# Identity matrix by a running sum, a matmul and a comparison, and reciprocal roots of two or three token tiles at once, in a one-core hybrid decoder step

## Chip, cores and metric

The kernel runs on one core of one Trainium2 chip. The metric is the device time of one execution in microseconds (us): 1366.59 us before, the median of 3 runs (1365.39 to 1371.83). One further execution was recorded by the hardware profiler; its trace is the source of all durations below. Engines: PE is TensorE (matmuls; PEld its weight loads), DVE is VectorE, ACT is ScalarE, POOL is GpSimd, SP is the queue that issues most DMAs.

## The reference, cut to what matters

One decoder layer over 1024 prompt tokens and 8 sample tokens of width 1024: an RMS norm, a wide input product, an S5 state-space branch and a convolution branch that are gated and merged, a SwiGLU feed-forward layer, and a last RMS norm.

```python
def rmsnorm(x, g):
    xf = x.astype(jnp.float32)
    y = xf * lax.rsqrt(jnp.mean(xf * xf, axis=-1, keepdims=True) + EPS)
    return (y * g.astype(jnp.float32)).astype(x.dtype)
...
    xn = rmsnorm(x, g_mix)
    z = xn @ w_in
    u = z[..., :D_SSM]
    ...
    y, hr, hi = s5_layer(u, h_re, h_im, a_re, a_im, log_dt, b_re, b_im, c_re, c_im, d)
    yg = jax.nn.gelu(y) @ w_glu
    ...
    x = x + merged @ w_out
    hn = rmsnorm(x, g_ffn) @ w_ff_in
    x = x + (jax.nn.silu(hn[..., :D_FF]) * hn[..., D_FF:]) @ w_ff_out
...
    return rmsnorm(x, g_final), ...
```

## The kernel before

**Tiles and stages.** The tokens stand in nine tiles `xt[0]` to `xt[8]`: eight of 128 tokens, and `xt[8]` with the 8 sample tokens. Products are made in float16 with a high and a low part of both sides (`wh`/`wl`, `xn` high and low), three matmuls for each. The stages by the profile: up to 84 us the first norm, the transposes of x and the product `u` (line 734, tile `pu`); then the rest of the input product together with S5 and the convolution branch; then the output product (line 1177), feed-forward (1291 and 1370), and from about 1331 us the last product (1391), a transposition of each token tile (1400) and the last norm.

**The order of work.** The program is recorded through a scheduler that simulates the engines and places each engine's instructions by readiness and priority (`hp()` raises it). The engines then run in that fixed order, each waiting for its own next instruction: a row of an engine that waits holds all rows behind it. Moving one dependency can so reorder rows of other parts.

**The identity.** `ident` is the first 128 columns of the tile `zi` (line 632 clears the rest). All transposes on TensorE multiply by it, and so wait for it. It was made by a library helper on GpSimd: a memset (masks.py:197) and an affine select (masks.py:199). `ones` (634) is a tile of ones, used by small matmuls that sum over partitions.

**The first norm.** `norm(ks)` squares each tile of a group on ScalarE with a running sum in a column of `ss` (705), makes a reciprocal root with `rsqrt` on VectorE (three scaled copies `rv` of the sum, a first guess `ry` by integer arithmetic, three rounds of Newton's method through `rt`: lines 615 to 626), and scales the tile (710 on VectorE for x0 and x1, 712 on ScalarE for the others). It is called for (0), (1), (2, 3), (4, 5) and (6, 7, 8). `xpose` transposes a group (724, tile `ptr`) and splits it into high and low halves of `xn` (608 on ScalarE, 609 on VectorE).

**The first weights.** `wscale_pe` takes the sums of squares of two weight tiles (516), adds them up on TensorE (546, `pws`) and makes a power of two `usc` (501) of it, with which `wsplit16` splits the weights (561 on ScalarE, 565 on VectorE). `raw` has two tiles at its first call. Later weights get their scale by an all-reduce over partitions on GpSimd (521, result `sv` read at 526 on VectorE).

**S5's loads.** `load_a` loads `ldt`, the step sizes, and `an`; `load_b` loads `cn`, `B`, `dn`, `h0n`; all are issued by GpSimd. `B` holds the same data in partitions 0 to 63 and 64 to 127: the upper half was copied from the lower. `prep(0)` makes an exponential of `ldt` on VectorE (lines 53 to 66, tiles `ex_x`, `ex_m`, `ex_p`).

**The last norm.** In three groups of token tiles (5 to 8, 0 to 2, 3 and 4), each tile in turn is transposed into `tr` (a PSUM pool with three buffers), squared with its sum (1403), given a reciprocal root of its own, and multiplied by that and the gain into `yo` (1410), which is stored.

Of the kernel before, what the change touches and what calls it, by code (L numbers as in the profile page):

```python
# [8 lines left out]

F32 = mybir.dt.float32  # L10
# [4 lines left out]
AF = mybir.ActivationFunctionType  # L15
ALU = mybir.AluOpType
MUL, ADD, SUB, MAXI, MINI = ALU.mult, ALU.add, ALU.subtract, ALU.max, ALU.min

P = 128
D = 1024  # L20
# [16 lines left out]
class S5:  # L37
# [54 lines left out]
    def load_b(self, dma):  # L92
        self.cn = []
        for i, c in enumerate((self.c_re, self.c_im)):
            t = self.t([P, 4, 2, NS], "^cn", tag="W", bufs=2)
            src = c[0].rearrange("(q g) c p -> (g c) q p", q=4)
            for r in range(2):
                dma.dma_start(t[:, :, r], src)
            self.cn.append(t)
        self.B = []  # L100
        for i, b in enumerate((self.b_re, self.b_im)):
            t = self.t([P, G, 16], f"B{i}")
            dma.dma_start(t[0:64], b[0].rearrange("g p c -> p g c"))
            dma.dma_start(t[64:128], t[0:64])
            self.B.append(t)
        self.dn = self.t([16, 512], "dn")
        dma.dma_start(self.dn, self.d[0:1, :].to_broadcast([16, 512]))
        self.h0n = self.t([P, 2, 3, NS], "^h0n", tag="E", bufs=2)
        for i, h in enumerate((self.sre, self.sim, self.sre)):
            dma.dma_start(self.h0n[:, :, i], h[0].rearrange("(q s) g p -> (s g) q p", q=2))  # L110
# [330 lines left out]
def hybrid_step(ctx: ExitStack, tc: tile.TileContext, x_prompt, x_sample, state_ssm_re, state_ssm_im,  # L441
# [4 lines left out]
    nc = tc.nc  # L446
    V, A, T, GP, SY = nc.vector, nc.scalar, nc.tensor, nc.gpsimd, nc.sync
# [3 lines left out]
    yk = y_p[0].rearrange("(j k) d -> k j d", k=8)  # L451
    xsm, ysm = x_sample[:, 0, :], y_s[:, 0, :]

    cp = ctx.enter_context(tc.tile_pool(name="cp", bufs=1))
    wp = ctx.enter_context(tc.tile_pool(name="wp", bufs=3))
    pa = ctx.enter_context(tc.tile_pool(name="pa", bufs=NA))
    ms = ctx.enter_context(tc.tile_pool(name="ms", bufs=2, space=bass.MemoryType.PSUM))
# [8 lines left out]
    def nm(s):  # L466
        uid[0] += 1
        return f"{s}_{uid[0]}"

    def sa(name, shape=(P, TOK), dt=F32):  # L470
        return pa.tile(list(shape), dt, name=nm(name), tag="a")

    def sb(name, shape=(P, TOK), dt=F32, tag="b"):
        return (pm if tag == "mg" else pb).tile(list(shape), dt, name=nm(name), tag=tag, bufs=NBT[tag])

    def hp():
        return tc.high_priority(offset=HPO)
# [36 lines left out]
    def sumsq(src, junk, o):  # L514
        with nc.allow_low_precision(reason="bound of a scale"):
            A.activation(junk, src, AF.Square, accum_out=o)  # L516
# [23 lines left out]
    def wscale_pe(raws, his):  # L540
        with tc.high_priority(offset=HPS):
            ss = cp.tile([P, 2], F32, name=nm("uss"), tag="uss", bufs=2)
            pt = pst.tile([P, 512], F32, name=nm("pws"), tag="pu")
            for i, raw in enumerate(raws):
                sumsq(raw, his[i].bitcast(BF16), ss[:, i:i + 1])
                T.matmul(pt[:, 0:1], ones, ss[:, i:i + 1], start=(i == 0), stop=(i == len(raws) - 1))
            v = cp.tile([P, 1], F32, name=nm("uv"), tag="uv", bufs=2)
            V.tensor_scalar(v, pt[:, 0:1], 1e-28, None, MAXI)
            o = cp.tile([P, 1], F32, name=nm("usc"), tag="usc", bufs=2)
            pow2(v, o, "pyw")  # L550
        return o
# [52 lines left out]
    def pair(t):  # L604
        return t[:, 0], t[:, 1]
# [5 lines left out]
    def rsqrt(ss, n, scale, r=P):  # L611
        v = cp.tile([P, 3, 9], F32, name=nm("rv"), tag="rv", bufs=2)[:r, :, :n]
        y = cp.tile([P, 9], I32, name=nm("ry"), tag="ry", bufs=3)[:r, :n]
        t = cp.tile([P, 9], F32, name=nm("rt"), tag="rt", bufs=2)[:r, :n]
        V.tensor_scalar(v[:, 0], ss, 64 * scale, 64 * EPS, MUL, ADD)
        V.tensor_scalar(y, v[:, 0].bitcast(I32), -0.5, -550020641.0, MUL, ADD)
        V.tensor_scalar(v[:, 1], ss, 16 * scale, 16 * EPS, MUL, ADD)
        V.tensor_scalar(v[:, 2], ss, 4 * scale, 4 * EPS, MUL, ADD)
        f = y.bitcast(F32)
        for i in range(3):  # L620
            if n == 1:
                V.scalar_tensor_tensor(t, f, f, v[:, i], MUL, MUL)
            else:
                V.tensor_tensor(t, f, f, MUL)
                V.tensor_tensor(t, t, v[:, i], MUL)
            V.scalar_tensor_tensor(f, t, -3.0, f, ADD, MUL)
        return f

    zi = cp.tile([P, 240], F32, name="zi")
    ident = zi[:, :P]  # L630
    make_identity(nc, ident)
    GP.memset(zi[:, P:], 0.0)
    ones = cp.tile([P, P], F32, name="ones")
    GP.memset(ones, 1.0)

    e5, e5c, e5t, est = ExitStack(), ExitStack(), ExitStack(), ExitStack()
    sp = e5.enter_context(tc.tile_pool(name="s5p", bufs=1, side="right"))
# [5 lines left out]
    xt = [None] * 9  # L643

    xn = []
    for _ in range(8):
        t = sa("xn", (P, 2, TOK), F16)
# [21 lines left out]
    raw = [wdma(w_in, 0, 8, P * m) for m in range(2)]  # L669
# [7 lines left out]
    pt = ms.tile([P, 512], F32, name="pgv", tag="ms")  # L677
# [10 lines left out]
    pt = ms.tile([P, 512], F32, name="pgm", tag="ms")  # L688
# [7 lines left out]
    def norm(ks):  # L696
        n = len(ks)
        with hp():
            ss = cp.tile([P, 3], F32, name=nm("ss"), tag="ss", bufs=2)
            if 8 in ks:  # L700
                GP.memset(ss, 1.0)
            junk = px.tile([P, D], BF16, name=nm("junk"), tag="junk", bufs=1)
            for i, k in enumerate(ks):
                r = P if k < 8 else 8
                A.activation(junk[:r], xt[k][:r], AF.Square, accum_out=ss[:r, i:i + 1])
            for i, k in enumerate(ks):
                r = P if k < 8 else 8
                f = rsqrt(ss[:, i:i + 1], 1, 1.0 / D)
                if k < 2:
                    V.tensor_scalar(xt[k], xt[k], f, None, MUL)  # L710
                else:
                    A.mul(xt[k][:r], xt[k][:r], f[:r])

    def cols(gr):
        return gr[0] * P, sum(P if k < 8 else 8 for k in gr)
# [42 lines left out]

    norm((0,))
    norm((1,))  # L760
    pairs = [wpair(), wpair()]
    wus = [wscale_pe(raw, [p[0] for p in pairs])]
    wui = [invs(wus[0], gxc[:, 1:2], "uinv", 2)]
    wu = [wsplit16(raw[0], *pairs[0], wus[0], parts=4)]
    xpose(groups[0])
# [6 lines left out]
    pairs = [[kt_(t, bufs=2) for _ in range(2)] for t in ("cosi", "M")]  # L772
# [163 lines left out]
    for m in range(4):  # L936
        t = sb("gyt")
# [100 lines left out]
    for c in range(3):  # L1038
        pt = ms.tile([P, 512], F32, name=nm("pmu"), tag="ms")
# [14 lines left out]
    for m in range(4):  # L1054
        a = acc[m]
# [19 lines left out]
    x1 = [None] * 8  # L1075
# [43 lines left out]
    for m in range(4):  # L1119
        h, l = pair(sb("chp", (P, 2, TOK), F16, tag="gy"))  # L1120
# [231 lines left out]
    for b in range(len(blocks) - 1):  # L1352
# [6 lines left out]
        for m in range(8):  # L1359
# [4 lines left out]
            for h in range(2):  # L1364
                pt = qpsum()
                for k in range(blocks[b]):
                    for q, (u, v) in enumerate(((0, 0), (0, 1), (1, 0))):
                        for z in range(2):
                            c0 = 516 * h + 258 * z
                            T.matmul(pt[:, z, :258], w[u][:, k], hid[k][v][:, c0:c0 + 258],  # L1370
                                     start=(k == 0 and q == 0), stop=(k == blocks[b] - 1 and q == 2))
# [9 lines left out]
    gf = sb("gf", (P, D), tag="gy")  # L1381
    SY.dma_start(gf, g_final[None, :].to_broadcast([P, D]))
    emq.close()
    tr = ctx.enter_context(tc.tile_pool(name="tr", bufs=3, space=bass.MemoryType.PSUM))
    for gr in ((5, 6, 7, 8), (0, 1, 2), (3, 4)):
        c0, w = cols(gr)
        for m in range(8):
            pt = ms.tile([P, 512], F32, name=nm("pfo"), tag="ms")
            for k in range(nb):
                for i, (a, b) in enumerate(((0, 0), (0, 1), (1, 0))):  # L1390
                    T.matmul(pt[:, :w], wl[m][a][:, k], hid[k][b][:, c0:c0 + w],
                             start=(k == 0 and i == 0), stop=(k == nb - 1 and i == 2))
            with hp():
                V.scalar_tensor_tensor(x1[m][:, c0:c0 + w], pt[:, :w], iwl[:, m // 2:m // 2 + 1], x1[m][:, c0:c0 + w],
                                       MUL, ADD)
        for k in gr:
            r = P if k < 8 else 8
            pt = tr.tile([P, 2, 512], F32, name=nm("tr"), tag="tr")
            for m in range(8):
                T.transpose(pt[:r, m // 4, (m % 4) * P:(m % 4 + 1) * P], x1[m][:, k * P:k * P + r], ident)  # L1400
            yo = sb("yo", (P, D))
            ss = cp.tile([P, 1], F32, name=nm("ss"), tag="ss", bufs=2)
            A.activation(yo[:r].rearrange("p (a b) -> p a b", a=2), pt[:r, 0:2], AF.Square,
                         accum_out=ss[:r, 0:1])
            f = rsqrt(ss[:r, 0:1], 1, 1.0 / D, r)
            dst = yk[k] if k < 8 else ysm
            step = 1 if k in (3, 4) else 2
            for h in range(0, 2, step):
                c = slice(512 * h, 512 * (h + step))
                V.scalar_tensor_tensor(yo[:r, c].rearrange("p (a b) -> p a b", a=step), pt[:r, h:h + step], f[:r, 0:1],  # L1410
                                       gf[:r, c].rearrange("p (a b) -> p a b", a=step), MUL, MUL)
                SY.dma_start(dst[:, c], yo[:r, c])


NA = 21
# [33 lines left out]
```

## Time and profile before

| | |
|---|---|
| median of 3 runs | 1366.59 us |
| the profiled execution | 1366.18 us |
| its span in the trace | 1364.1 us |
| granted TensorE clock, mean | 0.975 |
| instructions of the profile's VectorE | 2402 |
| loaded and stored by DMA | 96.66 MB |

The span runs from the first to the last recorded instruction; the execution's own time is 2.1 us longer. In the rows below a line number is that of the kernel before. `<-` between tiles reads "made from"; at the end of a row in brackets stands the idle time before it and what ended it. "issue" is time in which an engine waited for nothing that the profile shows. In the row of a DMA issue the last number is the time from issue to landing.

### The profile page before, as it was taken

The numbers are of one execution on the slowest core, as the hardware profiler recorded it, in microseconds if no ns is written. First come the engines' busy times: TensorE is split into PE (matmuls) and PEld (weight loads), VectorE is DVE, ScalarE is ACT, GpSimd is POOL, SyncE is SP. The second block draws the span as 40 slices with busy tenths as digits, with TensorE's granted clock in tenths as the row PEclk, the third lists the DMA queues.
The fourth block names the chain that finished last, engine by engine and source line by source line (L and its number), as shares of the span: only waits on it lengthen the run. The fifth ranks groups of instructions, "written<-read, shape, count | busy, mean of one in ns | idle before, by whom it ended". The sixth has DMA issues, their size and how long they took to land.

```text
span 1364.1 us, 25399 instructions
## 1 busy us (share of the span) xinstructions
PE 1263.1 (93%) x10083; PEld 1001.7 (73%) x10083; DVE 1036.5 (76%) x2402; ACT 621.6 (46%) x1118; POOL 102.8 (8%) x198
## 2 busy tenths in 40 slices
PE   3898797999998999799979999999999999999996
PEld 2776565666666666578658888888888888888884
DVE  5976788989997744768897857776785777678758
ACT  5843433453333545744354534444453544445522
POOL 5000012001110100000000000000000000000100
PEclk9899898999999999999979999999999999999998
DMA  6445665341122123410011121112112111221203
GB/s 190 130 97 120 135 113 119 81 127 50 48 62 63 30 82 98 135 32 1 17 41 46 40 78 48 40 55 68 50 39 78 48 39 55 68 58 32 77 18 125
DMA packets 169632, 96.66 MB, mean 71 GB/s; under 512 B 12927, under 2 KB 165643, under 8 KB 169513
## 3 DMA queue, kind: packets, MB, share of 16 engines
q1 hardware_dynamic: 168109, 92.44, 24.8%
q0 software_dynamic: 896, 1.63, 0.6%
q8 instruction: 79, 1.29, 0.4%
q10 hardware_dynamic: 507, 0.97, 0.3%
q14 instruction: 41, 0.33, 0.1%
HBM read 76.72 MB, written 9.65 MB: 63 GB/s over the span
## 4 chain that ended last, share of the span: by engine, by line
PE 51%; DVE 26%; issue 9%; DMA 8%; ACT 4%; POOL 1%; SPq 1%; DVEq 0%; ACTq 0%; POOLq 0%
PE q L1291 18%; PE q L1370 12%; PE mm L594 10%; PE q L1177 5%; DMA wr<-in_w_ff_in_dram 5%; DVE acc L898 4%; PE pu L734 2%; DVE ws L1249 2%; DVE wl L565 2%; DVE tb L898 1%; DMA Y<-X 1%; POOL sv L521 1%; ACT ws L1248 1%; DVE g L1270 1%; DVE mh L609 1%
## 5 line engine op out<-in xcount | busy, mean ns | idle before, releaser
L1291 PE MATMUL q<-xs,ws 128*128 128x258 f16 (+2 forms) x3696 | 422.6, 275 | 18.7 <-DVE xs L1225 6.7
L1291 PEld LDWEIGHTS <-ws 128*128 128x128 f16 x3696 | 358.4, 98 | 81.7 <-issue 24.6
L594 PEld LDWEIGHTS <-wh 128*128 128x128 f16 x1728 | 169.5, 98 | 86.2 <-issue 5.1
L594 PE MATMUL mm<-xn,wh 128*128 128x344 f16 (+2 forms) x1152 | 203.8, 311 | 1.9 <-ACT ut L746 1.1
L1370 PE MATMUL q<-hp,wh 128*128 128x258 f16 x1280 | 193.5, 272 | 0.0
L521 POOL PARTITION_ALL_REDUCE sv<-wss x110 | 71.0, 646 | 936.0 <-ACT wh L516 510.7
L1370 PEld LDWEIGHTS <-wh 128*128 128x128 f16 x1280 | 124.0, 97 | 18.1
L561 ACT ACTIVATE wh<-wr,wsc 128x512 f16<-128x512 f32 (+1 forms) x76 | 70.0, 922 | 126.9 <-DVE wsc L501 122.6
L1370 PE MATMUL q<-hp,wl 128*128 128x258 f16 x640 | 122.5, 273 | 0.0
L594 PE MATMUL mm<-xn,wl 128*128 128x344 f16 (+2 forms) x576 | 118.0, 312 | 0.0
L594 PEld LDWEIGHTS <-wl 128*128 128x128 f16 x864 | 85.2, 99 | 41.3 <-issue 0.3
L516 ACT ACTIVATE wh<-wr 128x512 bf16<-128x512 f32 (+1 forms) x78 | 65.0, 833 | 107.6 <-PE q L1370 44.6
L516 ACT ACTIVATE junkw<-wr 128x1024 bf16<-128x1024 f32 x52 | 54.8, 1054 | 109.2 <-DMA wr<-in_w_ff_in_dram 101.6
L565 DVE SCALAR_TENSOR_TENSOR wl<-wr,wsc,wh 128x512 f16<-128x512 f32 (+1 forms) x76 | 75.9, 999 | 22.6 <-ACT wh L561 22.4
L1374 DVE SCALAR_TENSOR_TENSOR x<-q,inv,x 128x516 f32<-128x516 f32 x80 | 59.9, 750 | 35.8 <-PE q L1370 35.6
L1177 PE MATMUL q<-mh,wo 128*128 128x258 f16 x672 | 80.0, 275 | 7.5 <-ACT mh L608 4.2
L1249 DVE SCALAR_TENSOR_TENSOR ws<-sw,wsc,ws 128x512 f16<-128x512 f32 x88 | 64.7, 744 | 19.4 <-ACT ws L1248 18.4
L1177 PEld LDWEIGHTS <-wo 128*128 128x128 f16 x672 | 64.3, 96 | 19.9 <-issue 7.6
L1248 ACT ACTIVATE ws<-sw,wsc 128x512 f16<-128x512 f32 x88 | 62.3, 715 | 28.9 <-PE q L1291 28.8
L1370 PEld LDWEIGHTS <-wl 128*128 128x128 f16 x640 | 61.9, 97 | 9.0
L594 PE MATMUL mm<-gyp,wh 128*128 128x344 f16 x384 | 66.6, 309 | 1.4 <-DVE mg L971 0.8
L1249 DVE SCALAR_TENSOR_TENSOR ws<-wr,wsc,ws 128x512 f16<-128x512 f32 x66 | 48.7, 744 | 17.9 <-ACT ws L1248 17.6
(404 smaller groups left out, 1852.8 us busy)
## 6 DMA issues: line engine op xcount, KB each, us to landing
wr<-in_w_ff_in_dram SPq DMA_DIRECT2D x44, 512.0 KB
wr<-in_w_in_dram SPq DMA_DIRECT2D x28, 512.0 KB
wr<-in_w_ff_out_dram SPq DMA_DIRECT2D x44, 256.0 KB
xt<-in_x_prompt_dram SPq DMA_DIRECT2D x8, 512.0 KB
cosi<-pc SPq DMA_DIRECT2D x32, 128.0 KB
wr<-in_w_glu_dram SPq DMA_DIRECT2D x16, 256.0 KB
wr<-in_w_out_dram SPq DMA_DIRECT2D x8, 512.0 KB
xc<-in_x_prompt_dram SPq DMA_DIRECT2D x8, 512.0 KB
```

The lines of the kernel that those rows point to most:

```text
L516: A.activation(junk, src, AF.Square, accum_out=o)
L521: GP.partition_all_reduce(v, ss, P, RMAX)
L561: A.mul(hi, raw, s)
L565: V.scalar_tensor_tensor(lo[:, sl], raw[:, sl], s, hi[:, sl], MUL, SUB)
L594: T.matmul(pt[:, c, :b - a], ww[:, k], aa[:, a:b], start=(k == 0 and i == 0), stop=(k == n - 1 and i == 2))
L898: V.scalar_tensor_tensor(o[:, q:], x[:, 0:HT - q], w[q], o[:, q:], MUL, ADD)
L1177: T.matmul(o, wo[m][u][:, k], cset(mh[k][v], j), start=(k == 0 and q == 0), stop=(k == 7 and q == 2))
L1248: A.mul(w[:, 0], src, s)
L1249: V.scalar_tensor_tensor(w[:, 1], src, s, w[:, 0], MUL, SUB)
L1291: T.matmul(o[:, z, :w_], w[:, u, k * P:(k + 1) * P], xs[k][i][:, v, c, a:b], start=(k == 0 and q == 0), stop=(k == 3 and q == 2))
L1370: T.matmul(pt[:, z, :258], w[u][:, k], hid[k][v][:, c0:c0 + 258], start=(k == 0 and q == 0), stop=(k == blocks[b] - 1 and q == 2))
L1374: V.scalar_tensor_tensor(x, pt[:, :, :258], inv, x, MUL, ADD)
```

## The change

1. The identity is no longer made by the helper on GpSimd. VectorE fills `ones`, and makes `jr` with a running sum along the free axis, so that column j of every row holds j + 1. A matmul of the first row of `jr` with a single one turns that row into a column `pj` (row i holds i + 1), VectorE copies it to `jc` and compares: `ident` is 1 where `jr` equals `jc`.
2. Both halves of `B` are loaded from DRAM.
3. The first norm makes one `rsqrt` for all tiles of a group. With one column it has 10 VectorE instructions, with two or three 13 (the product of a Newton round needs two instructions then).
4. The last norm does so for the pairs (5, 6), (7, 8) and (0, 1); tiles 2, 3 and 4 stay single.
5. `raw[:2]` in the first call of `wscale_pe` names the two tiles that `raw` has at that place.

```diff
-            dma.dma_start(t[64:128], t[0:64])
+            dma.dma_start(t[64:128], b[0].rearrange("g p c -> p g c"))
...
-    make_identity(nc, ident)
     GP.memset(zi[:, P:], 0.0)
     ones = cp.tile([P, P], F32, name="ones")
-    GP.memset(ones, 1.0)
+    V.memset(ones, 1.0)
+    with tc.tile_pool(name="jp", bufs=1) as jp:
+        jr = jp.tile([P, P], F32, name="jr")
+        V.tensor_tensor_scan(jr, ones, ones, 0.0, MUL, ADD)
+        pj = ms.tile([P, 512], F32, name="pj", tag="ms")
+        T.matmul(pj[:, 0:1], jr[0:1, :], ones[0:1, 0:1], start=True, stop=True)
+        jc = jp.tile([P, 1], F32, name="jc")
+        V.tensor_copy(jc, pj[:, 0:1])
+        V.tensor_scalar(ident, jr, jc, None, ALU.is_equal)
...
+            f = rsqrt(ss[:, :n], n, 1.0 / D)
             for i, k in enumerate(ks):
                 r = P if k < 8 else 8
-                f = rsqrt(ss[:, i:i + 1], 1, 1.0 / D)
                 if k < 2:
                     V.tensor_scalar(xt[k], xt[k], f, None, MUL)
                 else:
-                    A.mul(xt[k][:r], xt[k][:r], f[:r])
+                    A.mul(xt[k][:r], xt[k][:r], f[:r, i:i + 1])
...
-    wus = [wscale_pe(raw, [p[0] for p in pairs])]
+    wus = [wscale_pe(raw[:2], [p[0] for p in pairs])]
...
-        for k in gr:
...
-            f = rsqrt(ss[:r, 0:1], 1, 1.0 / D, r)
...
+        for sub in {5: ((5, 6), (7, 8)), 0: ((0, 1), (2,)), 3: ((3,), (4,))}[gr[0]]:
+            pts, yos = [], []
+            ss = cp.tile([P, 3], F32, name=nm("ss"), tag="ss", bufs=2)
...
+            for i, k in enumerate(sub):
...
+                A.activation(yo[:r].rearrange("p (a b) -> p a b", a=2), pt[:r, 0:2], AF.Square,
+                             accum_out=ss[:r, i:i + 1])
...
+            f = rsqrt(ss[:, :len(sub)], len(sub), 1.0 / D)
+            for i, k in enumerate(sub):
...
+                    V.scalar_tensor_tensor(yo[:r, c].rearrange("p (a b) -> p a b", a=step), pt[:r, h:h + step],
+                                           f[:r, i:i + 1], gf[:r, c].rearrange("p (a b) -> p a b", a=step), MUL, MUL)
```

The scheduler's order changes with it at three places. Line numbers of the changed kernel are one lower up to line 630 and six higher behind the identity. Numbers behind a tile's name count its buffers.

On GpSimd, at the start of the program, before the change; `ISA` is an instruction that configures the engine, and the select needs it:

```order
L634 MEMSET ones 128x128
L88 DMA ldt<-in_ssm_log_dt_dram 128x32
masks.py:199 ISA
masks.py:199 AFFINE_SELECT zi<-zi 128x128
L90 DMA an<-in_ssm_a_re_dram 32x2x64
L90 DMA an<-in_ssm_a_im_dram 32x2x64
```

The same place in the changed program, with the end of GpSimd's first rows:

```order
L87 DMA ldt<-in_ssm_log_dt_dram 128x32
L102 DMA B_142<-in_ssm_b_re_dram 64x32x16
L103 DMA B_142<-in_ssm_b_re_dram 64x32x16
L102 DMA B_145<-in_ssm_b_im_dram 64x32x16
L103 DMA B_145<-in_ssm_b_im_dram 64x32x16
L106 DMA dn<-in_ssm_d_dram 16x512
...
L897 MEMSET t_170_2362 128x1
L520 ISA
L520 ISA sv_1989<-wss_1987 128x1
```

The configuration ahead of the loads is gone and the loads of `B` stand first; the loads of `an`, `cn`, `h0n` and `cwn` follow later. One configuration is left at this end of the queue, directly ahead of the first all-reduce (the second of the two lines L520); before there was another at the first all-reduce too.

On VectorE, the first rows before the change:

```order
L685 TENSOR_REDUCE gmt<-gv 8x1
L680 COPY gt<-pgv 128x8
L686 TENSOR_SCALAR gmt<-gmt 8x1
L687 TENSOR_SCALAR gmt<-gmt 8x1
L615 TENSOR_SCALAR rv_291<-ss_288 128x1
L617 TENSOR_SCALAR rv_291<-ss_288 128x1
```

And rows 1 to 9 of the changed program (the second is the running sum):

```order
L632 MEMSET ones 128x128
L635 SCALAR_TENSOR_TENSOR jr<-ones 128x128
L639 COPY jc<-pj 128x1
L640 TENSOR_SCALAR zi<-jr,jc 128x128
L691 TENSOR_REDUCE gmt<-gv 8x1
L52 TENSOR_SCALAR ex_x<-ldt 128x32
L686 COPY gt<-pgv 128x8
L692 TENSOR_SCALAR gmt<-gmt 8x1
L54 TENSOR_SCALAR ex_m<-ex_x 128x32
```

The first step on `ldt` moved from row 11 to row 6, ahead of the copy of `gt` and of the first norm. Further down, the S5 steps that need `an` moved behind the splits of the weights, and the row that reads the first all-reduce (`sv`, line 525) moved from row 155 to row 112.

On ScalarE, around the split of the first weights, before the change (712 scales a tile of x, 705 squares one, 561 splits weights):

```order
L516 ACTIVATE wu_489,uss_493<-wr_390 128x1024
L712 ACTIVATE xt_119<-xt_119,ry_407 128x1024
L608 ACTIVATE xn_102<-ptr_360,gt 128x256
L705 ACTIVATE junk_403,ss_402<-xt_125 128x1024
L561 ACTIVATE wh_322<-wr_121,usc_334 128x1024
L561 ACTIVATE wh_324<-wr_123,usc_334 128x1024
L608 ACTIVATE xn_103<-ptr_365,gt 128x256
```

The same place in the changed program:

```order
L515 ACTIVATE wu_486,uss_490<-wr_397 128x1024
L607 ACTIVATE xn_109<-ptr_367,gt 128x256
L560 ACTIVATE wh_329<-wr_128,usc_341 128x1024
L560 ACTIVATE wh_331<-wr_130,usc_341 128x1024
L607 ACTIVATE xn_110<-ptr_372,gt 128x256
L607 ACTIVATE xn_111<-ptr_377,gt 128x256
L711 ACTIVATE junk_410,ss_409<-xt_132 128x1024
```

The scale of x2 left this place (it now stands ten rows further down) and the square of x3 moved behind both splits.

More of the change, by code (lines that the diff above doesn't have):

```diff
@@ L6 @@
 from concourse import mybir
-from concourse.masks import make_identity
 from concourse._compat import with_exitstack
@@ L1395, in hybrid_step @@
                                        MUL, ADD)
-        for k in gr:
[L1397 to L1404, printed above, removed]
-            f = rsqrt(ss[:r, 0:1], 1, 1.0 / D, r)
[L1406 to L1412, printed above, removed]
+        for sub in {5: ((5, 6), (7, 8)), 0: ((0, 1), (2,)), 3: ((3,), (4,))}[gr[0]]:
+            pts, yos = [], []
+            ss = cp.tile([P, 3], F32, name=nm("ss"), tag="ss", bufs=2)
+            if 8 in sub:
+                GP.memset(ss, 1.0)
+            for i, k in enumerate(sub):
+                r = P if k < 8 else 8
+                pt = tr.tile([P, 2, 512], F32, name=nm("tr"), tag="tr")
+                for m in range(8):
+                    T.transpose(pt[:r, m // 4, (m % 4) * P:(m % 4 + 1) * P], x1[m][:, k * P:k * P + r], ident)
+                yo = sb("yo", (P, D))
+                A.activation(yo[:r].rearrange("p (a b) -> p a b", a=2), pt[:r, 0:2], AF.Square,
+                             accum_out=ss[:r, i:i + 1])
+                pts.append(pt)
+                yos.append(yo)
+            f = rsqrt(ss[:, :len(sub)], len(sub), 1.0 / D)
+            for i, k in enumerate(sub):
+                r = P if k < 8 else 8
+                pt, yo = pts[i], yos[i]
+                dst = yk[k] if k < 8 else ysm
+                step = 1 if k in (3, 4) else 2
+                for h in range(0, 2, step):
+                    c = slice(512 * h, 512 * (h + step))
+                    V.scalar_tensor_tensor(yo[:r, c].rearrange("p (a b) -> p a b", a=step), pt[:r, h:h + step],
+                                           f[:r, i:i + 1], gf[:r, c].rearrange("p (a b) -> p a b", a=step), MUL, MUL)
+                    SY.dma_start(dst[:, c], yo[:r, c])
```

## Prediction, made before the changed kernel was run

> **What bounds the kernel now.** The page comes first, for the span, the busy shares and the chain that ended last.
>
> ```profile
> span 1364.1 us, 25399 instructions
> ...
> PE 1263.1 (93%) x10083; PEld 1001.7 (73%) x10083; DVE 1036.5 (76%) x2402; ACT 621.6 (46%) x1118; POOL 102.8 (8%) x198
> ...
> PE 51%; DVE 26%; issue 9%; DMA 8%; ACT 4%; POOL 1%; SPq 1%; DVEq 0%; ACTq 0%; POOLq 0%
> ```
>
> TensorE is idle for 1364.1 − 1263.1 = 101 us. Only a change that reaches those gaps, or delays TensorE, is seen in the time. Next come the waits, TensorE's first and then GpSimd's, and the first long piece of the chain in order of time:
>
> ```profile
> PE pgv L678 <- POOL zi masks.py:199: 14.2, 1, 14.2
> ...
> POOL zi masks.py:199 <- issue: 11.7, 1, 11.7
> ...
> 2.36 11.51 issue
> ```
>
> TensorE's longest wait is its first: 14.2 us for the identity, which GpSimd finishes late because it stands still for 11.51 us ahead of the affine select. The stages tell what that is worth. The columns of the windows are length, then busy time and count of PE, PEld, DVE, ACT and POOL, the granted clock, the DMA share and GB/s.
>
> ```profile
> 0.00:14.50 14.50, 0.27 (x1) 0.18 (x1) 0.27 (x1) 4.73 (x7) 2.17 (x10) 1.00 0.93 261
> 14.50:27.00 12.50, 6.53 (x25) 4.76 (x26) 11.55 (x90) 8.28 (x15) 12.21 (x18) 1.00 0.46 126
> 27.00:54.00 27.00, 22.54 (x151) 17.80 (x149) 26.08 (x124) 22.56 (x45) 5.91 (x18) 0.87 0.55 166
> 54.00:84.00 30.00, 30.00 (x262) 25.92 (x263) 27.88 (x103) 17.35 (x34) 0.00 (x0) 1.00 0.23 63
> 84.00:110.00 26.00, 21.66 (x162) 15.91 (x160) 14.19 (x27) 12.04 (x27) 1.17 (x10) 1.00 0.62 137
> 110.00:300.00 190.00, 167.75 (x1132) 121.16 (x1133) 158.50 (x314) 73.47 (x165) 22.72 (x41) 0.95 0.53 118
> 300.00:450.00 150.00, 142.91 (x945) 95.09 (x944) 138.04 (x255) 60.19 (x75) 16.16 (x15) 0.97 0.18 52
> 450.00:1320.00 870.00, 840.45 (x7200) 698.71 (x7198) 626.63 (x1371) 413.17 (x736) 42.50 (x90) 0.99 0.19 54
> ```
>
> For 14.5 us only ScalarE and the transfers work. From 14.5 to 54 VectorE is the bound (37.63 of 39.5 us busy), then TensorE (30.00 of 30.00 up to 84, 840 of 870 later). Work is chained through all of them, so an earlier start can travel to the end.
>
> **The identity.** What is late once the affine select is gone? Rows of the timeline, start and duration first, and from the view of the transfers one with its time from issue to landing:
>
> ```profile
> 1.35 0.86 POOL L88 DMA_DIRECT2D ldt<-in_ssm_log_dt_dram  x1
> 13.88 0.28 POOL masks.py:199 TENSOR_SCALAR_AFFINE_SELECT zi<-zi 128x128 f32<-128x128 f32 x1 [11.67 <-issue]
> ...
> 14.52 0.17 DVE L680 COPY gt<-pgv 128x8 f32<-128x8 f32 x1 [12.08 <-PE pgv L678]
> ...
> 17.65 0.75 DVE L710 TENSOR_SCALAR xt<-xt,ry 128x1024 f32<-128x1024 f32 x1
> ...
> 5.58 0.19 ACT L705 ACTIVATION_READ_ACCUMULATOR junk<-xt 128x1 f32 x1
> ...
> ldt<-in_ssm_log_dt_dram POOLq DMA_DIRECT2D x1, 16.0 KB, 7.7
> ```
>
> The five new VectorE and TensorE steps have no row of their own. The nearest rows run from 0.17 us (the copy of 128x8) to 0.75 us (128x1024, eight times the new 128x128). Four VectorE steps and a small matmul are then between 0.85 and 3.75 us, 5 us at most from the start. None of it is on the path: in the new order VectorE's row 6 is `ex_x<-ldt`, ahead of everything that the first norm needs, and `ldt` lands at 1.35 + 7.7 = 9.05. So VectorE goes on at 9.05 instead of 14.52: **−5.5 us**. If `ldt` came sooner, the first sum of squares, which ScalarE has at 5.58 + 0.19 = 5.8, would allow up to 3 us more; if it came later behind the new B loads, as much less.
>
> **Order up to the first u matmul.** Before, the scales of the first weights were ready on VectorE, but ScalarE first finished other things:
>
> ```profile
> 23.04 0.14 DVE L501 TENSOR_SCALAR usc<-py 128x1 int32<-128x1 int32 x1
> ...
> 23.04 1.15 ACT L712 ACTIVATE xt<-xt,ry 128x1024 f32<-128x1024 f32 x1
> 24.08 0.47 ACT L608 ACTIVATE xn<-ptr,gt 128x256 f16<-128x256 f32 x1
> 24.43 1.06 ACT L705 ACTIVATE junk<-xt 128x1024 bf16<-128x1024 f32 x1
> ...
> 25.47 2.19 ACT L561 ACTIVATE wh<-wr,usc 128x1024 f16<-128x1024 f32 x2
> ...
> 26.48 1.06 PE L252 MATMUL pc<-zi,cn 128*128 128x128 f32 x4
> 27.33 0.42 PE L734 MATMUL pu<-xn,wh 128*128 128x256 f16 x1
> ```
>
> One rsqrt for x2 and x3 needs both squares, so the scale of x2 (1.15 us) leaves its place and the square of x3 falls behind the two splits. ScalarE can split `wh` when `usc` is there (23.18) plus little, not at 25.47. That is 2.3 us, and with the `pc` transposes, which no longer stand ahead in TensorE's queue, about **−2.4 us**; between 0, if x1's norm is then the late one, and −3. The first u matmul comes at 27.33 − 7.9 = 19.4.
>
> **Fewer rsqrt instructions.** One tile takes 10 VectorE instructions, two or three take 13. The first norm falls from 9 x 10 = 90 to 2 x 10 + 3 x 13 = 59. Between 14.52 and 17.65 VectorE starts 27 instructions, 0.116 us each; 31 fewer are 3.6 us of an engine that is the bound up to 54. Only those ahead of the weight splits move TensorE, and beyond 54 TensorE is full, so I take **−1.0**, between 0 and −3.6. The end of the u stage has a check of its own: TensorE is busy for 22.54 + 30.00 us from 27 to 84, so from 19.4 it can end at 72 at the earliest, 12 us before now; with the gaps it has today, 8. My 8.9 lies inside.
>
> **B loaded twice from DRAM.** Four transfers stand on GpSimd's queue right behind `ldt`, instead of two loads and two copies at 29 us.
>
> ```profile
> B<-B POOLq DMA_DIRECT2D x2, 128.0 KB, 5.0
> ...
> B<-in_ssm_b_re_dram POOLq DMA_DIRECT2D x1, 128.0 KB, 4.6
> B<-in_ssm_b_im_dram POOLq DMA_DIRECT2D x1, 128.0 KB, 5.6
> ```
>
> They meet the x and weight loads of the first window (DMA share 0.93). At its 261 GB/s the 512 KB are 2 us. I take 0, as x0 and x1 are issued earlier, and +2 as the other end. The Trainium skill ("DMA: Bandwidth & Descriptors", Specifications) speaks against this edit: it wants 512 B at least for line rate, and these pieces have 64 B. The trace puts 4.6 and 5.6 us of the small-piece loads beside 5.0 of the copy between on-chip rows, so I see no penalty of that size here.
>
> **The first all-reduce.** GpSimd's standstill was at an instruction of configuration. The new order keeps one such, but at the first all-reduce:
>
> ```profile
> 31.18 0.12 POOL L1195 MEMSET st<- 128x3 f32 x2
> 37.89 0.98 POOL L521 PARTITION_ALL_REDUCE sv<-wss  x1 [6.58 <-ACT wh L516]
> ```
>
> GpSimd needed 31.18 − 14.13 = 17 us for its loads and small work behind the select. From 2.2 on, with two more loads and slower landings, it reaches the first all-reduce between 19 and 24, and a standstill of 11.51 us ends between 31 and 36. Its result is wanted by VectorE at `sv`, row 112 of the new order. The 106 rows from `ex_x` on, at 26.08 / 124 = 0.21 us (window 27 to 54), are 22 us, so VectorE gets there at 31 to 32. The price lies between 0 and +4. I take 0: GpSimd's 17 us from 2.2 on, without longer waits, give 19, and 19 + 11.5 is in time. The Trainium skill ("GPSIMD Engine Reference", Instruction dispatch) gives about 6 us for a first call to newly loaded code. By it the result would be there before 31 and the price is 0; the trace shows 11.51 for the first, and for the second at most the 6.58 ahead of this row.
>
> **The final norm.** Groups of VectorE by form between 1331 and 1361, and the last rows of the timeline:
>
> ```profile
> L1410 DVE SCALAR_TENSOR_TENSOR yo<-tr,ry,gf 128x1024 f32<-128x1024 f32 x6 | 7.7, 1281 | 0.0
> ...
> 1354.96 1.02 ACT L1403 ACTIVATE yo<-tr 128x1024 f32<-128x1024 f32 x1 [2.45 <-issue]
> ...
> 1356.11 0.15 DVE L615 TENSOR_SCALAR rv<-ss 128x1 f32<-128x1 f32 x1 [1.02 <-ACT yo L1403]
> ...
> 1359.27 1.41 DVE L1410 SCALAR_TENSOR_TENSOR yo<-tr,ry,gf 128x512 f32<-128x512 f32 x2
> ```
>
> Three pairs make 60 instructions 39; 21 at 0.1 are −2 us of VectorE. Against it, the first product of a pair waits for the second square (1.02 us), and both PSUM buffers of a pair are held until then, with three in all. Tiles 3 and 4, which end the kernel, stay single. Placing the rows by hand, the last product starts 0.2 later than without the edit: **+0.2**, between −2 and +2.
>
> **Sum.** −5.5 − 2.4 − 1.0 + 0.2 = −8.7. The profiled execution took 1366.18 us (its span and 2.1 around it), 0.4 under the median of 1366.59. 1366.18 − 8.7 = **1357.5 us**. About 0.5%, 6.8 us, is what a measurement of this kernel can tell from no change; faster by that begins at 1359.8.
>
> **Rivals.** *Part of the gain is taken back between 84 and 450* by stages that wait for something else: TensorE has 4.3 + 22.3 + 7.1 = 33.7 us of gaps there, and the preparation for S5 (exponentials, sine and cosine) now stands behind the weight splits. For it: 158.50 of 190 us of VectorE up to 300, so a late row costs. Against: nothing in these stages has a fixed time. Half of 8.7 is left: 1362. *A larger gain*: the u stage ends 12 us earlier, as bounded above, and the waits up to 450 shrink by a few us more: 1352 to 1354. *The change doesn't do what it says*: VectorE, at row 6, is held about as long as before, because `ldt` now lands with the crowd of B loads near 14: 1365 or 1366. Its 7.7 us in a crowd already speak for a part of it. *Slower*: the first all-reduce holds VectorE. Everything behind `sv`, row 112, has to wait, the x copies and the S5 preparation among them, and TensorE runs dry as soon as the rows ahead of it are used up. It decides if GpSimd reaches the configuration after 38 instead of 24: then the result comes at 50, VectorE loses 50 − 32 = 18 us, and −8.7 turns into about +9: 1375. For it: GpSimd's loads wait for landings in turn. Against: 14 us more than worked out.
>
> **Chances.** Forecast, 1355 to 1360: 0.52. Half taken back, 1360 to 1364: 0.22. Larger gain, 1350 to 1355: 0.13. No effect, 1364 to 1367: 0.07. Slower, about 1375: 0.06. Faster by over 0.5% is 0.13 and nearly all of 0.52: 0.63; within 0.5%: 0.31; slower: 0.06. The range, 1350 to 1365.5, leaves out the slow case and most of the one without effect. The bounds of the costs, −5.5 − 3 − 3.6 − 2 = −14 and −5.5 + 2 + 4 + 2 = +2.5, lie a little outside it on both sides; all ends together are not likely.
>
> **What would show it.** Right: TensorE's first wait ends well before 9, VectorE's longest early wait names the DMA `ldt` and ends near 9; the first u matmul is near 19.4, the last of the stage between 72 and 76; the last product starts 8 to 9 us earlier. Wrong: `ldt` landing after 11; a wait of `sv` on GpSimd of more than 3 us near 32; TensorE's gaps between 84 and 450 above 36 us in sum; a pair in the tail that leaves VectorE idle for more than 2 us.

## The result: 0.93% slower

The changed kernel takes 1379.11 us (median of 6 runs, 1374.99 to 1380.43), the kernel before 1366.80 us in 6 runs beside it: a ratio of 1.0093, 95% interval 1.0076 to 1.0110, 12 to 13 us more. The forecast was 1357.5 us; the time lies outside the range, on the side of the slower rival, but by another mechanism. The profiled execution of the changed kernel took 1379.60 us. From its page, the span and the busy times:

```profile
span 1377.5 us, 25338 instructions
...
PE 1265.7 (92%) x10085; PEld 1003.2 (73%) x10085; DVE 1034.6 (75%) x2354; ACT 622.4 (45%) x1118; POOL 96.5 (7%) x196
```

The engines have almost the same work as before (TensorE 2.6 us more, VectorE 1.9 less). The span grew by 13.4 us, so it is mostly waiting that grew. The windows of the changed kernel, cut as before (length, then busy time and count of PE, PEld, DVE, ACT and POOL, clock, DMA share, GB/s):

```profile
0.00:14.50 14.50, 3.60 (x13) 2.67 (x13) 6.82 (x49) 5.45 (x8) 8.23 (x15) 1.00 0.94 187
14.50:27.00 12.50, 5.50 (x25) 3.65 (x24) 4.70 (x15) 7.69 (x15) 8.83 (x14) 1.00 0.98 240
27.00:54.00 27.00, 21.89 (x171) 17.69 (x169) 22.15 (x107) 22.99 (x42) 1.67 (x12) 0.94 0.59 181
54.00:84.00 30.00, 30.00 (x262) 25.89 (x263) 28.21 (x113) 18.88 (x42) 1.98 (x3) 1.00 0.14 38
84.00:110.00 26.00, 18.89 (x137) 13.32 (x135) 13.76 (x28) 9.56 (x22) 1.72 (x12) 0.94 0.66 136
110.00:300.00 190.00, 164.72 (x1106) 119.04 (x1107) 157.70 (x309) 72.41 (x161) 22.85 (x35) 0.94 0.53 117
```

VectorE's work starts in the first window, as forecast. But from 14.5 to 27 it is busy for 4.70 us only, where it was busy for 11.55, and TensorE does 18.89 + 164.72 us between 84 and 300 where it did 21.66 + 167.75. The start, in the timelines of VectorE, ScalarE, TensorE and GpSimd (start, duration, row, and in brackets the idle time before it with what ended it):

```profile
2.33 0.29 DVE L640 TENSOR_SCALAR zi<-jr,jc 128x128 f32<-128x128 f32 x1
...
8.10 0.18 DVE L52 TENSOR_SCALAR ex_x<-ldt 128x32 f32<-128x32 f32 x1 [5.25 <-DMA ldt<-in_ssm_log_dt_dram]
...
13.00 0.75 DVE L716 TENSOR_SCALAR xt<-xt,ry 128x1024 f32<-128x1024 f32 x1
21.29 0.48 DVE L608 SCALAR_TENSOR_TENSOR xn<-ptr,gt,xn 128x256 f16<-128x256 f32 x1 [7.53 <-ACT xn L607]
...
19.74 1.06 ACT L515 ACTIVATE wh<-wr 128x1024 bf16<-128x1024 f32 x1 [4.81 <-DMA wr<-in_w_in_dram]
...
24.48 0.39 PE L740 MATMUL pu<-xn,wh 128*128 128x256 f16 x1
...
34.31 0.35 POOL L520 PARTITION_ALL_REDUCE sv<-wss  x1 [4.72 <-ACT wh L515]
```

The identity is ready at 2.6 and x1 is scaled at 13.75 (20.35 before). Then VectorE waits 7.53 us for ScalarE, whose next row but one squares the second weight tile, and that tile lands only just before 19.74. Before, that row ran at 16.29 and didn't wait for the tile. The first u matmul comes at 24.48, 2.85 us earlier than before, not 7.9.

Further on, the last u matmul, the first S5 product (`px`) and S5's last (`py`) in TensorE's timeline, first before and then after:

```profile
91.27 0.50 PE L734 MATMUL pu<-xn,wu 128*128 128x264 f16 x3
...
110.10 1.87 PE L355 MATMUL px<-U,E 128*128 128x136 f32 x8 [3.32 <-DMA U<-uds]
...
256.80 0.40 PE L395 MATMUL py<-U,M 128*128 128x136 f32 x2
```

```profile
88.06 0.50 PE L740 MATMUL pu<-xn,wu 128*128 128x264 f16 x3
...
110.39 2.15 PE L354 MATMUL px<-U,E 128*128 128x136 f32 x8 [5.34 <-DMA U<-uds]
...
263.46 0.40 PE L394 MATMUL py<-U,M 128*128 128x136 f32 x2
```

The last u matmul ends 3.2 us earlier than before, the first S5 product starts no earlier, and S5's last ends 6.7 us later. The output product then starts 10.5 us later (574.68 against 564.20), so 3.8 us more are lost between these two, and the other 2.9 of the 13.4 behind it, most of them in the last norm (below). Where those 3.8 are lost is open.

Waits of VectorE and TensorE in the changed kernel (in total, times, longest):

```profile
DVE pc L323 <- DMA uds<-ut: 12.1, 1, 12.1
...
DVE X L365 <- DMA cosi<-pc: 8.0, 1, 8.0
...
PE pe L300 <- ACT xs L358: 7.0, 1, 7.0
...
PE px L354 <- DMA U<-uds: 5.3, 1, 5.3
```

Before, the longest waits of these lines were 5.3 (line 323 is 324 there) and 6.1 us (for `Y`) on VectorE and, on TensorE, 0.6 (`pe`, for `xs`) and 3.3. The rows of SP's queue tell more. S5 needs three things over this one queue: the rotation tables `cosi`, made by VectorE and stored in four pieces a table, the matrix `M`, loaded back from DRAM after `kvd` was written there, and `U`. Around the first `M` before:

```profile
98.91 0.60 SPq L337 DMA_DIRECT2D cosi<-pc  x1
99.56 0.59 SPq L338 DMA_DIRECT2D cosi<-pc  x1
100.34 0.64 SPq L316 DMA_DIRECT2D M<-kvd  x1
101.02 1.27 SPq L751 DMA_DIRECT2D ud<-ut  x1
```

and after:

```profile
92.10 1.31 SPq L336 DMA_DIRECT2D cosi<-pc  x1
93.52 0.53 SPq L484 DMA_DIRECT2D wr<-in_w_in_dram  x1
95.13 0.66 SPq L315 DMA_DIRECT2D M<-kvd  x1
95.89 1.71 SPq L337 DMA_DIRECT2D cosi<-pc  x1
...
100.89 0.61 SPq L337 DMA_DIRECT2D cosi<-pc  x1
105.67 0.63 SPq L757 DMA_DIRECT2D ud<-ut  x1
107.14 0.37 SPq L843 DMA_DIRECT2D U<-ud  x1
```

In the chain of before, `M` needed 7.37 us from issue to landing:

```profile
100.34 7.37 DMA M<-kvd
```

There all eight pieces of the first two tables stood ahead of it; in the changed order one does, and seven stand behind. The last stores of u and the loads of `U` stand behind `M` in both orders; the first load of `U` is issued at 105.77 before and at 107.14 now, though the u stage ended 3.2 us earlier. What the pieces hold up is line 323. It begins the next two tables in the tile `pc`, of which the kernel has one buffer, so it has to wait until all eight pieces are stored from it. That row before and after:

```profile
102.29 0.69 DVE L324 TENSOR_TENSOR pc<-ec 128x512 f32<-128x512 f32 x1 [5.32 <-DMA cosi<-pc]
```

```profile
108.35 0.69 DVE L323 TENSOR_TENSOR pc<-ec 128x512 f32<-128x512 f32 x1 [12.07 <-DMA uds<-ut]
```

(The profile puts the second wait down to a store of u on the same queue, behind the pieces and `M`; which of them ended it, the trace can't tell.) The third table is late in turn: its last piece is issued at 138.22, right behind the second `M` at 137.55, and VectorE, which needs this table, stands still for 8.0 us until 147.77. Before, its four pieces were issued by 129.68, and VectorE took that step at 138.12. (The expectations below count two pieces ahead of the first `M` where it is one, and nine before where it is eight.)

### The profile page after: what moved, and what is told of

Same layout as the page of the kernel before. It is cut to its first block, busy times and chain, and to the rows that moved or that the text cites. A ratio compares the mean times of both kernels' runs of the same rounds, so it can differ in the third digit from the quotient of the medians.

```text
span 1377.5 us, 25338 instructions
## 1 busy us (share of the span) xinstructions
PE 1265.7 (92%) x10085; PEld 1003.2 (73%) x10085; DVE 1034.6 (75%) x2354; ACT 622.4 (45%) x1118; POOL 96.5 (7%) x196
## 5 line engine op out<-in xcount | busy, mean ns | idle before, releaser
L520 POOL PARTITION_ALL_REDUCE sv<-wss x110 | 65.1, 592 | 951.4 <-ACT wh L515 540.0
```

The costliest lines, as they stand in the source:

```text
L520: GP.partition_all_reduce(v, ss, P, RMAX)
```

## Experiments

Seventeen kernels, one of them timed twice, each in several rounds beside the kernel before on the same chip. That kernel's median lay between 1359.6 and 1361.3 us on these chips, against 1366.8 above, so ratios are compared; 0.1% is 1.4 us.

**The parts alone.** Each is the kernel before with one part of the change: the identity with `ones` on VectorE; the line of `B`; the first norm; the last norm.

> The kernel before with the new identity alone (B, both norms as before). Theory A (the new identity lets the scheduler put S5's loads and preparation later, and S5's start pays for it): slower than before by 4 to 9 us, 1371 to 1376, the first u matmul near 22, S5's first product (px) not earlier than before's 110.1. Rival B (the identity's gain travels to the end, and the loss in the changed kernel is due to the other edits): faster by 3 to 6 us, 1361 to 1364, px near 105.

> The kernel before with both halves of B loaded from DRAM alone. There the four loads follow the old identity and do not meet the first x and weight loads. If the loads cost only where they meet those: no change within 2 us of 1366.8, first u matmul at 27.3 as before. If they cost by themselves: 3 us or more slower.

> The kernel before with one reciprocal root per group in the first norm alone. Theory A gives 0 to -3 us, the first u matmul 1 to 2.4 us earlier than 27.3 (the scale of x2 leaves the place ahead of the weight splits). Rival: the moved rows cost S5's preparation as much as in the changed kernel, +3 us or more.

> The kernel before with the pairs in the last norm alone. Theory A (a pair holds two of three PSUM buffers and the tail loses 2.5 us, as the two traces show from the last product to the end): 1369, +2 to +3 us, everything before 1330 as in the kernel before. Rival (the tail of the changed kernel was only shifted by what came ahead): 0 within 1 us.

| part alone | ratio to before, 95% interval | us |
|---|---|---|
| identity | 1.0000 (0.9990 to 1.0010) | 0 |
| B | 0.9999 (0.9989 to 1.0008) | 0 |
| first norm by groups | 1.0043 (1.0029 to 1.0057) | +6 |
| last norm by pairs | 1.0023 (1.0015 to 1.0032) | +3 |

The identity alone moves the first u matmul to 21.73, 5.6 us ahead of before, and its first `px` to 106.74, 3.4 us ahead, and brings nothing at the end: neither the gain of rival B nor the loss of theory A came. In the first norm the rival was right (the first u matmul comes 1.4 us earlier, as theory A told, but the total is 6 us longer), in the last norm theory A. The norms cost, B is free where it doesn't meet the first loads. The sum is 9 us, so something is missing.

**Two parts, and the change without one.** First identity and B together, then the change with `B`'s copy as before:

```diff
-            dma.dma_start(t[64:128], b[0].rearrange("g p c -> p g c"))
+            dma.dma_start(t[64:128], t[0:64])
```

> The new identity and both halves of B from DRAM, both norms as before. Theory A (alone neither costs anything, together the four loads of B in 64-byte pieces stand beside the first x and weight loads and delay the second weight tile): the sum of squares of the second weight tile near 19.7 as in the changed kernel (15.96 with the identity alone), first u matmul near 24.5, total 3 to 5 us above before. Rival (the remaining 4 us come from the norms meeting the new order): within 1.5 us of before.

> The changed kernel with the copy inside B as before. Theory A: what is left is the first norm (+5) and the last norm (+3), so +8 us over before, 4 us less than the changed kernel; second weight tile's squares near 16, first u matmul near 20 to 21.5. Rival: +12, as changed.

Identity and B: 1.0082 (1.0059 to 1.0106), +11 us, from two parts that cost nothing alone. Change without B: 1.0093 (1.0068 to 1.0118), as slow as with it, though its second weight tile is squared at 16.27 and its first u matmul comes at 21.00, as expected. The mechanism on the transfers is right in both runs, its price at the end in neither. The second weight tile in ScalarE's timeline, with identity and B, then with the identity alone:

```profile
20.09 1.06 ACT L515 ACTIVATE wh<-wr 128x1024 bf16<-128x1024 f32 x1 [4.49 <-DMA wr<-in_w_in_dram]
```

```profile
15.96 1.06 ACT L515 ACTIVATE wh<-wr 128x1024 bf16<-128x1024 f32 x1 [0.91 <-DMA wr<-in_w_in_dram]
```

The window from 9 to 16 us (its last two columns are the DMA share and GB/s), with identity and B, with the identity alone, and before:

```profile
9.00:16.00 7.00, 2.97 (x10) 2.00 (x10) 5.45 (x45) 2.30 (x4) 0.83 (x2) 1.00 1.03 110
```

```profile
9.00:16.00 7.00, 2.39 (x8) 1.50 (x8) 5.23 (x41) 1.92 (x5) 2.53 (x7) 1.00 1.09 193
```

```profile
9.00:16.00 7.00, 1.24 (x5) 1.14 (x5) 1.02 (x12) 1.91 (x3) 2.11 (x4) 1.00 1.04 332
```

With four loads of B in pieces of 64 bytes the transfer engines are busy throughout and move 110 GB/s, with two 193, with none at that time 332. The weight tile is 4.1 us later for it. The loads of B themselves, which landed after 4.6 and 5.6 us before, take this long in the changed kernel (the last number, a median of two):

```profile
B<-in_ssm_b_re_dram POOLq DMA_DIRECT2D x2, 128.0 KB, 11.8
B<-in_ssm_b_im_dram POOLq DMA_DIRECT2D x2, 128.0 KB, 13.0
```

The loss at the end doesn't follow from that.

**The place of the running sum.** `jr` stood in a pool that is given back, and the scheduler then put the loads into that space (`an`, `cn`) behind B's. Here it borrows the first norm's scratch tile, alone with the identity and in the whole change:

```diff
-    with tc.tile_pool(name="jp", bufs=1) as jp:
-        jr = jp.tile([P, P], F32, name="jr")
...
+    jr = px.tile([P, D], BF16, name="jr", tag="junk", bufs=1)[:, :2 * P].bitcast(F32)
```

> The new identity alone, but its running sum stands in a buffer of the first norm's scratch tile instead of a pool that is given back, so that the loads of an and cn are in their old place ahead of B. Theory A (identity's gain of 5.6 us at the first u matmul is lost in part because S5's preparation is put later): faster than before by 3 to 7 us, px near 103 or earlier. Rival (S5's start is set by the transfers behind the u stage on SP's queue, whatever the preparation does): within 1.5 us of the identity alone, which was equal to before.

> The changed kernel, with the running sum in that scratch buffer: B's four loads then stand behind an and cn. Theory A: B's pieces still meet the second weight tile, a little later; +5 to +9 us over before instead of +12.5. Rival (order of S5's preparation does not matter): +12.

Identity so: 1.0051 (1.0031 to 1.0071), 7 us slower than with the pool. The whole change so: 1.0164 (1.0137 to 1.0191), +22 us. A miss in both. `an` and `cn` stand in their old places, but more small loads now meet the weights (the squares of the second tile at 19.02 and 22.98). The u stage ends 6.5 us later than with the identity alone (94.14), and 8.5 later than in the changed kernel (97.03), about as much as the ends lose against those two (7 and 10 us). So these runs don't tell what the order of S5's loads is worth.

**SP's queue.** The changed kernel, the identity alone and the kernel before, with the stores of `cosi` at raised priority. Then the changed kernel with `kvd`'s store and `M`'s load issued by GpSimd:

```diff
+                with self.tc.high_priority(offset=HPO):
                     SY.dma_start(d[0:64], pv[64 * hi_:64 * hi_ + 64, 0:2, h])
                     SY.dma_start(d[64:128], pv[64 * hi_:64 * hi_ + 64, 0:3:2, h])
```

```diff
     def coef_m(self, m):
-        SY = self.nc.sync
+        SY = self.nc.gpsimd
```

> The changed kernel, with the DMAs of the rotation tables cosi at raised priority, so that on SP's queue all eight of the first two tables stand ahead of the first load of M (in the changed kernel two of eight do). Theory C (each M load takes 7 us to land, cosi pieces queued behind it hold VectorE's in-order rows, and S5's stage pays): VectorE's wait of 8 us for cosi before line 365 and of 12 us before line 323 shrink below 5 us each, S5's last py near before's 257 instead of 263.4, total +4 to +8 us over before. Rival D (S5 is late for its coefficients on VectorE, not for the queue): no better than +11.

> The new identity alone (equal to before when run) with cosi's DMAs at raised priority. Theory C: a few us faster than before, 2 to 5 us. Rival D: within 1.5 us.

> The kernel before with cosi's DMAs at raised priority alone; there nine of the first cosi pieces stand ahead of M already. Theory C: within 2 us of before. Rival D: the same, so this run is only the base for the other two.

> The changed kernel with the store of kvd and the load of M issued by GpSimd instead of SP, so that nothing on SP waits behind them. Theory C: +4 to +8 us over before, VectorE's two waits below 5 us. Rival D: +11 or more. A third way: GpSimd's descriptors are slow and its all-reduces wait, then sv waits grow on VectorE beyond the changed kernel's 52 us in sum.

| kernel | ratio to before, 95% interval | us |
|---|---|---|
| change, `cosi` first | 1.0061 (1.0046 to 1.0076) | +8 |
| identity, `cosi` first | 0.9997 (0.9985 to 1.0009) | 0 |
| before, `cosi` first | 0.9996 (0.9984 to 1.0007) | 0 |
| change, `M` on GpSimd | 1.0012 (1.0004 to 1.0021) | +2 |

Raising `cosi` gives back 4 of the 12.5 us, moving `M` 11, more than theory C's 4 to 8; the same two edits to the kernel before (the second below) give nothing, and with the identity alone raising `cosi` doesn't give theory C's 2 to 5 us either. With `cosi` first in the changed kernel the total is as told, the way to it is not: the wait at line 323 shrinks to 2.90 us, but it is 9.22 at the next pair of tables, another of 11.71 for a swap appears, and S5 ends at 261.3, not near 257. Waits of VectorE between 118 and 152 us, first of the changed kernel, then with `M` on GpSimd:

```profile
DVE X L365 <- DMA cosi<-pc: 8.0, 1, 8.0
DVE X L365 <- DMA Y<-X: 5.5, 1, 5.5
```

```profile
DVE Y L380 <- DMA X<-Y: 6.4, 1, 6.4
DVE X L365 <- DMA Y<-X: 2.1, 1, 2.1
```

The wait for `cosi` is gone, but another of 6.4 us for a swap takes part of its place (13.5 us in sum in the changed kernel, 8.5 here), which theory C's 5 us did not allow, and the wait at line 323 is 6.06 us. On GpSimd's queue `M` itself lands later than the 7.37 us of before, after a median of 9.9:

```profile
M<-kvd POOLq DMA_DIRECT2D x4, 512.0 KB, 9.9
```

So what S5 lacked wasn't `M`, but what stood behind it. TensorE is busy for 20.22 + 172.31 = 192.5 us between 84 and 300, where the changed kernel had 183.6 and the kernel before 189.4. The third way, more waiting for `sv`, didn't come: 54.1 us in sum. Nor is the loss one of the clock alone: the profiled execution with `M` on GpSimd has a mean granted clock of 0.968, the changed kernel's 0.969.

The wait at line 323 divides all the kernels that have `M` on SP. In six of them at least one of the first eight pieces stands behind the first `M`: the changed kernel, the change without B (one piece), identity and B (five), the first norm alone (one) and the two with the running sum in the scratch tile (three and seven). There it is 11.5 to 15.5 us, and all six lose 6 to 22 us. In the other seven no piece stands behind `M`, it is 0.5 to 5.7 us, and only the two with the pairs lose: the pairs alone 3 us, the change with `cosi` first 8. One piece is enough, as the tile is free only when the last is stored. The wait for the third table is no such sign. With B alone, which costs nothing, that step waits as long:

```profile
146.20 0.69 DVE L366 TENSOR_TENSOR X<-X,cosi 128x512 f32<-128x512 f32 x1 [8.68 <-DMA Y<-X]
```

**Is that gain the changed order's own?** `M` on GpSimd in other kernels: before; identity alone; the change with the last norm as before; identity and first norm; identity and B. The last but one is followed by a repetition of the second.

> The kernel before with kvd's store and M's load issued by GpSimd. Theory C (the M loads on SP hurt mainly where the order puts cosi pieces behind them, as in the changed kernel): 0 to -4 us, so that the 11 us which the same edit gave the changed kernel are mostly its own. Rival E (the edit helps any order alike): -9 to -11 us.

> The new identity alone with M issued by GpSimd. Theory C: with the queue out of the way the 5.6 us that the first u matmul comes earlier reach the end in part, -3 to -6 us against before. Rival E: -10 us; rival F (S5 has no use for an earlier start): equal to the kernel before with M on GpSimd.

> The changed kernel with M on GpSimd and the last norm tile by tile as before. Theory A (pairs cost 2.5 to 3 us at the end): 2 to 3.5 us less than with the pairs (+1.6 there), so -1 to -2 against before. Rival: no difference to +1.6.

> The new identity and the first norm by groups, M on GpSimd, B and the last norm as before. Theory A (B's four loads cost 3.4 us ahead of the first u matmul): first u matmul near 20.5 instead of 24.4, total 1 to 3 us less than the run that has B's loads as well. Rival: equal to it.

> The new identity and both halves of B from DRAM (together +11 us when run) with M issued by GpSimd. Theory C (the loss of that pair is the same: cosi pieces behind M on SP): within -3 to +3 us of before, 8 us or more given back; squares of the second weight tile still near 20. Rival: +8 or more, so that the pair loses by something else.

> The same kernel as id_m_on_gpsimd once more, on whatever chip: -1.5 to -5 us against before if that gain is real, 0 if it was chance.

| with `M` on GpSimd | ratio to before, 95% interval | us |
|---|---|---|
| kernel before | 0.9998 (0.9987 to 1.0009) | 0 |
| identity | 0.9977 (0.9967 to 0.9988) | −3 |
| identity, again | 0.9976 (0.9963 to 0.9989) | −3 |
| identity, B | 0.9986 (0.9972 to 1.0000) | −2 |
| change without the pairs | 0.9990 (0.9979 to 1.0001) | −1 |
| whole change (from above) | 1.0012 (1.0004 to 1.0021) | +2 |
| identity, first norm | 1.0025 (0.9996 to 1.0054) | unclear |

The kernel before gains nothing, so the 11 us are the changed order's own, and rival E falls. Identity and B, +11 us together on SP's queue, are at −2 here: theirs was the same loss, though the second weight tile is as late as ever (its squares at 20.48). On SP's queue that pair has its first `px` at 98.21, 11.9 us earlier than before, and its last `py` ends at 265.8, 8.6 later; with `M` on GpSimd these are 99.32 and 253.8. So the loss arises between them, and not by a late start of S5. The pairs cost the same 3 us as alone. The identity with `M` on GpSimd beats the kernel before in both timings, by 0.23% and 0.24%.

What the first norm costs here is open. The change without the pairs has it and is at 0.9990, identity and B lack it and are at 0.9986; but identity and first norm ran at about 1357 us in five of its twelve runs (granted clock 0.973 to 0.977) and at about 1370 in seven (0.965 to 0.972). Why the same program has two times is open; the only trace is of a run at 1356.28. A loss as large as the one to be explained can thus come with `M` off SP's queue too.

**The tail.** Why the pairs cost 3 us is in the trace. From the changed kernel's timelines of VectorE, TensorE and ScalarE:

```profile
1363.29 2.47 DVE L1425 SCALAR_TENSOR_TENSOR yo<-tr,ry,gf 128x1024 f32<-128x1024 f32 x2
...
1364.71 3.65 PE L1411 MATMUL tr<-zi,x 128*128 128x128 f32 x16 [3.69 <-DVE yo L1425]
...
1368.44 1.02 ACT L1413 ACTIVATE yo<-tr 128x1024 f32<-128x1024 f32 x1 [0.59 <-ACT yo L1413]
```

Tiles 0, 1 and 2 hold all three PSUM buffers. As 0 and 1 are a pair, neither is free before the first product at 1363.29, and the last transposes stand for 3.69 us. Before, that wait was at most 1.6 us. From the last square on, the chain is no longer than before (5.7 us from 1354.96 to the end of the last product there, 5.7 from 1368.44 here); it only starts later.

## Why the prediction was wrong

1. **Start, −5.5:** right, even a little too small. `ldt` was the next thing late, and VectorE went on at 8.10 where it had at 14.52 (−6.4). The identity's own steps were done at 2.62.
2. **Order up to the first u matmul, −2.4:** the order moved as told, the gain did not come, because the next thing late was neither VectorE nor ScalarE, but the landing of the second weight tile. The term that failed here is the one for **B, taken as 0 with +2 as the other end**. It cost 4.1 us at the second weight tile (15.96 without the four loads, 20.09 with them, in the pair of runs above) and 3.5 at the first u matmul (21.00 in the change without B, 24.48 with it). The other 1.6 us of the way to 19.4 are missing without B too. The prediction read the landing time of one load in the order of before, behind the first crowd (4.6 us, beside 5.0 for the copy), as a sign of its price; what a load takes away from others is told by the rate while the transfer engines are busy, 110 GB/s where 332 had been. The Trainium skill ("DMA: Bandwidth & Descriptors", Specifications) had said so: pieces under 512 bytes miss the line rate. The prediction set the rule aside on a row that didn't test it; here the trace agrees with the rule.
3. **First norm, −1.0:** wrong in sign, +6 alone. Alone it puts one piece of `cosi` behind `M`, and the wait at line 323 is 11.73 us, so the likely cause is the new order and not the saved instructions; no run with `M` off the queue settles it (above).
4. **From the u stage to the end, passed on in full:** the step that cost most. The prediction let the stage end 8.9 us earlier and carried that to the end, setting its rival aside with the words "nothing in these stages has a fixed time". The stage ended 3.2 us earlier. (Its end is not at 84 us, from where the prediction worked out its 72 to 76: the last u matmul of before ends at 91.77.) Even without B, where the first u matmul is 6.3 us earlier, the last is only 2.4 earlier, so part of the gain is lost in the stage itself; how, is open. The rest is lost behind it. S5 begins with transfers in one queue, in the order in which the scheduler wrote them down, one of them lands after 7.4 us, and a tile that VectorE needs comes free only when the pieces behind it are stored: 12.07 us of waiting at line 323 where it had been 5.32. The row of 7.37 us for `M` was in the trace of before. The prediction looked at the new order of GpSimd, VectorE and ScalarE (the three places named ahead of it), and not at SP's. Its rival of a gain taken back had the place (84 to 450, S5's preparation late) but the price of half the gain; from the last u matmul to S5's last product alone it was 3.2 + 6.7 = 9.9 us, more than all of it, and 3.8 more up to the output product.
5. **First all-reduce, 0:** right. GpSimd was there later than told (29.6, not 19 to 24), but idle for only 4.72 us before the all-reduce at 34.31, and no `sv` of this stage waited. So any standstill for the configuration was at most 4.72 us here, not the 11.51 of the program's start, and the slower rival fell with it. The Trainium skill ("GPSIMD Engine Reference", Instruction dispatch) gives some 6 us for a first call to newly loaded code; the bound measured here lies below it.
6. **Last norm, +0.2:** the mechanism was named (both buffers of a pair held until the second square), the size was off: +3. The placing by hand missed that the third group's transposes wait for the second group's pair.

What is shown: in the changed order 11 of the 12.5 us go away when `M` is issued on another queue, with identity and B all 11 do, and in the order of before the same edit gives nothing; every kernel with pieces of `cosi` behind the first `M` has the long wait at line 323 and loses time; B's loads delay the second weight tile. What is argued only: that this wait is the whole way by which the 11 us are lost. Taking the pieces from behind `M` gave back 4, and some 5 us beside the 3 of the pairs stayed. Moving `M` also reorders other rows, which no run here separates, and one kernel lost as much with `M` on GpSimd in seven of twelve runs.

## What to carry to other kernels

Where a scheduler writes the order, an edit's own cost may be small beside that of the order which it sets off: compare the new order of every queue, those that only issue transfers first, and look in each for a slow transfer that now stands ahead of something waited for, such as the last store out of a tile with one buffer. The landing time of a transfer on a quiet queue is not what it takes from others; ask what rate the engines keep while it runs. A gain at the start counts only up to the next stage that begins with a fixed chain of transfers.

## What was not expected of the hardware

GpSimd stood still for 11.51 us at the start of the program, ahead of its first affine select, and for at most 4.72 us ahead of the first all-reduce, in the middle of the other work. From 9 to 16 us the transfer engines were busy all the time and moved 332, 193 or 110 GB/s, with none, two or four loads in pieces of 64 bytes among the others. The kernel before gave medians from 1359.6 to 1366.8 us in this study, 7 us apart, which is over half of the loss explained here, and one kernel had two times 13 us apart on the same chip.
